# Other array shapes for four small matmuls, and scale, bias and gain in other places, in a hybrid RWKV-7 and Mamba-2 layer

## The chip, the cores and the metric

One core of one Trainium2 chip runs the whole program. The metric is the device time of one execution in microseconds, as the median over runs. The engines are TensorE (PE in the profile; its weight loads are PEld), VectorE (DVE), ScalarE (ACT), GpSimd (POOL) and SyncE (SP), whose queue issues the DMA transfers.

## The reference

One decoder layer runs over a prompt of 2048 tokens and eight sample tokens of 1024 features. All values are fp32.

```python
proj = x @ w_in                                   # 1024 -> 3336
pr = proj[..., :1792]; u = pr + (prev - pr) * mu  # prev: the row before
r, k, v, uw, ua, ug = split(u)                    # 3 x 512, 64, 64, 128
w_log = -softplus(-(w0 + tanh(uw) @ w_up)) - 0.5; decay = exp(-exp(w_log))
a = sigmoid(a0 + ua @ a_up); g = sigmoid(ug) @ g_up
# per head (8 heads of 64), step by step, S is the state:
S = S * w_t + (S @ ka_t) kb_t^T + v_t k_t^T;  y_t = S @ r_t
o_r = (group_norm(y) + sum(r * k * r_k) * v) * g
# Mamba-2: short convolution, dt = softplus(proj_dt + bias) with 8 heads,
# chunked scan, gate, RMS norm -> o_m
h = layer_norm(ALPHA * x + [o_r, o_m] @ w_out) * g1 + b1
y = layer_norm(ALPHA * h + square(relu(h @ w_ff1)) @ w_ff2) * g2 + b2
```

The states are outputs too.

## The kernel before

The prompt is cut into four blocks of 512 tokens; the sample rides with block 1. `project` multiplies a block by 27 tiles of `w_in`, 128 output features each and 8 for dt (`T_DT`). Weights and activations are split into a high part in fp32r and the rest (`split`: ACT copies, DVE or GpSimd subtracts), and `mm3` sums three fp32r matmuls: high by high, high by rest, rest by high. Small matmuls that are not split are plain fp32; the profile records each as two instructions. `pair` takes two heads through the low-rank projections and writes the scaled vectors to DRAM (`s_ar`, `s_bk`, `s_v`).

`mixers` then runs the recurrence in eight chunks of 64 steps per block. `rwkv` prepares one chunk: the score matmuls `pss` of `bk` and `ar` into two banks, one for each half of the partitions (four pairs of heads, two halves), a blocked inverse by `masked` and transposes, and the tiles `sc`, `xf`, `bt`, `uv`. `chain` carries the state `ST` from chunk to chunk: `pr` from scores by v plus `ar` by state, `pu`, then `pn`, `py` and the next state. `rwkv_post` and `mamba` do the rest of the mixing.

`tail` is the bulk of a block: the output projection in two halves (eviction L1257), the transposes `hT` of the normalised rows (L163) with `ln1` scale and bias (L1295, in ACT) and the split, then the MLP in `ff1` and the accumulation into `hs` (L1453). Two generators finish a block late: `late` normalises the old block and multiplies by the gain `ln2` (`gain`, L1175 and L1176, two DVE operations of 128x1024 for each of four row tiles, then the DMA to y_p), and `gain` does `ln1` for the rows that stay as the residual. `late` is stepped in the second half of the output projection and emptied ahead of the transposes.

`drive` mixes the bulk generators with the mixers of the next block by rates: mixers of block 0 run beside the projections of blocks 1 to 3, mixers of block b+1 beside the tail of block b. What is written in this order is only a priority: at build time a planner with a cost model places every instruction, each engine then runs its own list in order, and tiles come from pools with fixed numbers of buffers (`BUFS`; PSUM: three banks `psb`, one `psa`, two `psm`, one `psc`, one `psy`). `g4` holds the wide row tiles, the hidden tiles, the pair tiles and the gain vectors.

Of the kernel before, what the change touches and what calls it, by code (L numbers as in the profile page):

```python
# [18 lines left out]
FIRST = 4  # L19
POOLA, POOLO, POOLF = 4, 2, 0  # L20
# [6 lines left out]
BUFS = (("wr", 7), ("w", 8), ("act", 8), ("g4", 12), ("r", 2), ("blk", 4),  # L27
# [3 lines left out]
KT = 8  # L31
# [76 lines left out]
class K:  # L108
# [41 lines left out]
    def mm(self, out, l, r, start=True, stop=True):  # L150
        self.nc.tensor.matmul(out, l, r, start=start, stop=stop)  # L151
# [71 lines left out]
    def setup_mix(self):  # L223
# [51 lines left out]
        self.waup = c("waup", (128, 512))  # L275
        nc.sync.dma_start(self.waup, A["waup"])
# [49 lines left out]
    def wpieces(self, j, halves=(0, 1)):  # L326
        out = []
        w = TILES[j][1]
        for h in halves:
            if w == 128:  # L330
                src = self.A["w_in"][j if j < T_DT else j - 1, :, h * 512:(h + 1) * 512]
            else:
                src = self.A["w_dt"][:, h * 32:(h + 1) * 32]
            out.append(self.wpiece(src, (4, w)))
        return out

    def project(self, b, ahead):
# [13 lines left out]
        for j in range(NT):  # L351
            w = TILES[j][1]
            if b == 0 and j < len(self.first):
# [26 lines left out]
    def evict(self, b, j, mains):  # L380
        nc, st = self.nc, self.blkst[b]
        if j < T_DT:
# [22 lines left out]
            if j == T_UWA:  # L405
                nc.scalar.activation(u[0:64], u[0:64], AF.Tanh)
            elif j == T_UG:
# [11 lines left out]
        else:  # L419
            i = j - T_Z  # L420
            th = self.pair_tile()[0][:, :TB]
            for o, m, ps in mains:
# [4 lines left out]
                              th.rearrange("p (u t) -> p u t", u=4))  # L427

# [36 lines left out]
    def delta(self, b, mains):  # L465
        nc, st = self.nc, self.blkst[b]
        raw = self.pair_tile()[0]
        for o, m, ps in mains:
            nc.scalar.activation(raw[0:8, o:o + m], ps, AF.Copy)
        pt = self.ps("a", (128, 4, 8))  # L470
        for u in range(4):
            self.tr(pt[:, u, :], raw[0:8, u * 128:(u + 1) * 128])
        dt = self.sm("dt", [128, 4, 8], bufs=4)
        nc.vector.tensor_tensor(out=dt, in0=pt, in1=self.dtb.unsqueeze(1).to_broadcast([128, 4, 8]), op=ALU.add)
# [28 lines left out]
    def pair(self, b, hp):  # L503
# [22 lines left out]
        self.mm(pw, self.waup[0:64, cs], uwa[0:64])  # L526
        self.mm(pa, self.waup[64:128, cs], uwa[64:128])
# [15 lines left out]
        for u in range(4):  # L543
# [22 lines left out]
        nc.sync.dma_start(self.s_bk[b][:, 64:128, hp, :].rearrange("c p x -> p c x"),  # L566
                          BK[64:128].rearrange("p c a t -> p c (a t)"))
        for a in range(2):
            nc.sync.dma_start(self.s_bk[b][:, 0:64, hp, (1 - a) * 64:(1 - a) * 64 + 64].rearrange("c p x -> p c x"),
                              BK[0:64, :, a, :])  # L570
# [1007 lines left out]
```

## Time and profile before

| | us |
|---|---|
| median of three runs | 2901.62 (2898.83 to 2908.35) |
| the profiled execution | 2905.99 |
| its span, first to last instruction | 2904.2 |

The profiled execution is one run with the hardware profiler; the sums are made against its own time. Granted clock is the share of full speed that the throttle gave TensorE; its mean over the span was 0.985.

### The profile page before, as it was taken

How to read it: one execution, taken by the hardware profiler on the slowest of the kernel's cores; microseconds unless marked ns; L12 is line 12 of the kernel's file. 1: busy time of each engine (PE TensorE's matmuls, PEld its weight loads, DVE VectorE, ACT ScalarE, POOL GpSimd, SP SyncE). 2: the span in 40 equal slices, each digit the busy share in tenths (PEclk: the TensorE clock that was granted, in tenths of full speed). 3: DMA queues.
4: the chain of work that ended last, by engine and by line, in shares of the span. 5: the costliest groups of instructions: out<-in, count | busy, mean ns of one | idle time of the engine just before them, and what ended most of it. 6: DMA issues, size and time to landing. Idle time of an engine off the chain costs nothing.

```text
span 2904.2 us, 53242 instructions
## 1 busy us (share of the span) xinstructions
PE 2825.7 (97%) x19648; PEld 2331.7 (80%) x19648; DVE 1963.2 (68%) x4765; ACT 1249.2 (43%) x2391; POOL 356.6 (12%) x510
## 2 busy tenths in 40 slices
PE   9999999999999999999999999998999999899997
PEld 6798987777788777788888888887877878888886
DVE  6767868867857777686866666568766655754446
ACT  4454544543536333344544344335443334543332
POOL 2221212211221000001300000022000000300001
PEclk9999999999999999999999999999999999999999
DMA  6654654554645444355523344254343334433232
GB/s 191 182 174 122 176 179 139 165 175 136 178 144 162 129 124 119 114 160 176 175 89 106 116 122 120 76 174 165 114 137 110 108 106 162 164 99 94 91 100 71
DMA packets 334169, 395.34 MB, mean 136 GB/s; under 512 B 85518, under 2 KB 191588, under 8 KB 333900
## 3 DMA queue, kind: packets, MB, share of 16 engines
q1 hardware_dynamic: 333908, 391.94, 44.8%
q8 instruction: 154, 2.52, 0.4%
q14 instruction: 107, 0.88, 0.1%
HBM read 331.06 MB, written 60.81 MB: 135 GB/s over the span
## 4 chain that ended last, share of the span: by engine, by line
PE 83%; DVE 9%; DMA 4%; issue 2%; ACT 2%; SPq 0%; POOL 0%; DVEq 0%; ACTq 0%; POOLq 0%
PE psb L156 19%; PE psb L157 18%; PE psb L158 18%; PE psm L151 7%; PE psa L156 4%; PE psa L157 4%; PE psa L158 4%; PE psc L151 2%; PE psa L151 2%; PE psm L163 1%; PE psy L694 1%; PE psb L151 1%; DVE w L190 1%; DMA wr<-in_w_in_dram 1%; DVE g L1176 1%
## 5 line engine op out<-in xcount | busy, mean ns | idle before, releaser
L189 ACT ACTIVATE w<-wr 128x512 fp32r<-128x512 f32 (+1 forms) x840 | 521.0, 625 | 693.2 <-PE psb L158 272.3
L190 DVE TENSOR_TENSOR w<-wr,w 128x512 fp32r<-128x512 f32 x714 | 511.0, 722 | 255.7 <-ACT w L189 247.0
L156 PE MATMUL psb<-act,w 128*128 128x512 f32 (+3 forms) x1796 | 637.4, 356 | 5.7 <-ACT act L189 5.0
L157 PE MATMUL psb<-act,w 128*128 128x512 f32 (+3 forms) x1796 | 630.0, 351 | 0.0
L158 PE MATMUL psb<-act,w 128*128 128x512 f32 (+3 forms) x1796 | 628.3, 350 | 0.0
L156 PEld LDWEIGHTS psb<-act,w 128*128 128x128 f32 (+1 forms) x1796 | 337.9, 189 | 61.5 <-ACT act L189 6.3
L158 PEld LDWEIGHTS psb<-act,w 128*128 128x128 f32 (+1 forms) x1796 | 338.4, 189 | 51.4 <-issue 3.3
L157 PEld LDWEIGHTS psb<-act,w 128*128 128x128 f32 (+1 forms) x1796 | 339.1, 189 | 46.1 <-DVE act L190 1.3
L156 PE MATMUL psb<-w,g 128*128 128x512 f32 x788 | 315.7, 403 | 0.2 <-ACT w L189 0.2
L157 PE MATMUL psb<-w,g 128*128 128x512 f32 x788 | 312.4, 396 | 0.0
L158 PE MATMUL psb<-w,g 128*128 128x512 f32 x788 | 311.4, 395 | 0.0
L190 POOL TENSOR_TENSOR w<-wr,w 128x512 fp32r<-128x512 f32 (+1 forms) x126 | 181.5, 1445 | 564.6 <-ACT w L189 546.4
L1453 DVE TENSOR_TENSOR g<-psb,g 128x512 f32<-128x512 f32 x173 | 118.9, 688 | 158.2 <-PE psb L158 157.8
L156 PEld LDWEIGHTS psb<-w,g 128*128 128x128 f32 x788 | 148.0, 188 | 36.5 <-ACT w L189 0.6
L158 PEld LDWEIGHTS psb<-w,g 128*128 128x128 f32 x788 | 148.0, 188 | 34.5 <-issue 0.3
L157 PEld LDWEIGHTS psb<-w,g 128*128 128x128 f32 x788 | 148.4, 188 | 32.5 <-issue 0.2
L190 DVE TENSOR_TENSOR g<-r,g 128x256 fp32r<-128x256 f32 (+1 forms) x172 | 97.2, 565 | 87.4 <-ACT g L189 86.3
L1403 ACT ACTIVATE r<-psb 128x512 f32<-128x512 f32 (+2 forms) x130 | 63.3, 488 | 208.9 <-PE psb L158 205.7
L156 PE MATMUL psa<-act,w 128*128 128x256 f32 (+2 forms) x336 | 115.7, 344 | 0.0
L157 PE MATMUL psa<-act,w 128*128 128x256 f32 (+2 forms) x336 | 114.1, 340 | 0.0
L158 PE MATMUL psa<-act,w 128*128 128x256 f32 (+2 forms) x336 | 113.5, 338 | 0.0
L156 PE MATMUL psb<-g,w 128*128 128x264 f32 (+3 forms) x324 | 108.9, 336 | 1.2 <-DVE g L400 0.8
(376 smaller groups left out, 5237.2 us busy)
## 6 DMA issues: line engine op xcount, KB each, us to landing
wr<-in_w_ff_dram SPq DMA_DIRECT2D x512, 256.0 KB
wr<-in_w_in_dram SPq DMA_DIRECT2D x208, 256.0 KB
wr<-in_w_out_dram SPq DMA_DIRECT2D x112, 256.0 KB
lr<-d_l SPq DMA_DIRECT2D x256, 64.0 KB
s_m<-g SPq DMA_DIRECT2D x48, 256.0 KB
ms<-s_m SPq DMA_DIRECT2D x16, 768.0 KB
wr<-in_xT_dram SPq DMA_DIRECT2D x32, 256.0 KB
s_ar<-g SPq DMA_DIRECT2D x16, 512.0 KB
```

Source lines behind the costliest of these rows:

```text
L151: self.nc.tensor.matmul(out, l, r, start=start, stop=stop)
L156: nc.tensor.matmul(out, l[0], r[0], start=first, stop=False)
L157: nc.tensor.matmul(out, l[0], r[1], start=False, stop=False)
L158: nc.tensor.matmul(out, l[1], r[0], start=False, stop=last)
L163: self.nc.tensor.transpose(out, in_, self.cst[p0:p0 + k, o + p0:o + p0 + k])
L189: nc.scalar.activation(hi, raw, AF.Copy)
L190: (eng or nc.vector).tensor_tensor(out=lo, in0=raw, in1=hi.bitcast(F32), op=ALU.subtract)
L694: acc = lambda o, l, r, start, stop: nc.tensor.matmul(o, l, r, start=start, stop=stop, skip_group_check=True)
L1176: eng.tensor_tensor(out=h, in0=h, in1=b[:p], op=ALU.add)
L1403: nc.scalar.activation(rl, ps, AF.Relu)
L1453: self.nc.vector.tensor_tensor(out=h, in0=ps, in1=h, op=ALU.add)
```

## The change

- Low-rank projections: the weights `w_up` and `a_up` are held as two tiles each of 128 rows (the high part stacked on itself, the rest stacked on itself), the inputs as high part over rest (`stacked`), and `pair` sums two fp32r matmuls of 128 rows where it had one fp32 matmul of 64.
- dt: high part and rest of the eight weight columns stand side by side as 16 columns (`wdt`), so two matmuls a step do the work of three; `delta` adds the two groups of eight after the transpose. The sample adds them with one small matmul.
- Scores: the four times two matmuls go through `row`, which gives all but the first a high priority and ties each behind the one before; the first is placed behind a DVE memset of one element of the second bank (`held`), without a wait between the engines for it. The halves that `s_bk`, `s_v` and `sc` exchange are exchanged the other way round.
- pr: `ar` is copied into the free half of `sc` and the state into the free half of `uv`, and one matmul of 128 rows replaces two of 64 that were summed.
- Tail: odd k of the scale and bias are done by DVE. The old block's gain and output (`finish2`) leave `late` and are stepped as `later` ahead of the new block's gain, one step per `ff1`; the gain vectors of `ln1` are loaded after them. `g4` has 14 buffers for 12, in the room that a smaller DMA scratch leaves.

The diff, cut: the renamed halves, the sums in `delta` and the sample's own matmuls are left out.

```diff
-BUFS = (("wr", 7), ("w", 8), ("act", 8), ("g4", 12), ("r", 2), ("blk", 4),
+BUFS = (("wr", 7), ("w", 8), ("act", 8), ("g4", 14), ("r", 2), ("blk", 4),
...
+    def row(self, args, held):
+        prev = self.mm(*args[0])
+        self.tc.add_manual_dep(prev.ins, held.ins.name, mybir.DependencyInfo(
+            mybir.DependencyClass.NoSync, mybir.DependencyReason.DATA), reason="bank")
+        for a in args[1:]:
+            with self.tc.high_priority(RANK), self.tc.issue_after(prev.ins):
+                prev = self.mm(*a)
...
-        self.waup = c("waup", (128, 512))
-        nc.sync.dma_start(self.waup, A["waup"])
+        self.wup = []
+        for i in range(2):
+            raw = self.sb("wr", (128, 512))
+            for h in range(2):
+                nc.sync.dma_start(raw[64 * h:64 * h + 64], A["waup"][64 * i:64 * i + 64])
+            self.wup.append([self.mp.tile([128, 512], F32R, name=f"wup{i}{s}") for s in range(2)])
+            self.split(raw, *self.wup[i])
...
+    def wdt(self):
+        raw = self.sb("wr", (128, 512))[:, :64]
+        self.nc.sync.dma_start(raw, self.A["w_dt"])
+        t = self.sb("w", (128, 2, 512), F32R)[:, 0, :128].rearrange("p (k s c) -> p s k c", k=KT, s=2)
+        self.split(raw.rearrange("p (k c) -> p k c", k=KT), t[:, 0], t[:, 1])
+        return t.rearrange("p s k c -> p k s c")
...
-                    l = [pieces[k // 4][i][:, k % 4, :] for i in range(2)]
                     r = [act[k][:, i, o:o + n] for i in range(2)]
-                    self.mm3(ps[:w, :n], l, r, k == 0, k == KT - 1)
+                    if j == T_DT:
+                        l = pieces[:, k].rearrange("p s c -> p (s c)")
+                        self.mm(ps[:w, :n], l, r[0], k == 0, False)
+                        self.mm(ps[:w, :n], l, r[1], False, k == KT - 1)
+                    else:
+                        l = [pieces[k // 4][i][:, k % 4, :] for i in range(2)]
+                        self.mm3(ps[:w, :n], l, r, k == 0, k == KT - 1)
...
+    def stacked(self, u):
+        nc = self.nc
+        hl = self.sb("g4", (128, 2, 520), F32R)
+        W, a = hl[:, 0, :TB], hl[:, 1, :TB]
+        lo, hi = slice(0, 64), slice(64, 128)
+        for t, x, y in ((W, lo, hi), (a, hi, lo)):
+            nc.scalar.activation(t[x], u[x], AF.Copy)
+            nc.vector.tensor_tensor(out=t[y], in0=u[x], in1=t[x].bitcast(F32), op=ALU.subtract)
+        return W, a
...
         pw, pa = self.ps("a"), self.ps("b")
-        self.mm(pw, self.waup[0:64, cs], uwa[0:64])
-        self.mm(pa, self.waup[64:128, cs], uwa[64:128])
+        for p, w, x in ((pw, self.wup[0], uwa[0]), (pa, self.wup[1], uwa[1])):
+            self.mm(p, w[0][:, cs], x, True, False)
+            self.mm(p, w[1][:, cs], x, False, True)
...
         pss = [self.ps("m", (128, 4, 128)) for j in range(2)]
-        for hp in range(4):
-            for j in range(2):
-                self.mm(pss[j][:, hp, :], bk[H[j], hp, :], ar[H[j], hp].rearrange("p a t -> p (a t)"))
+        held = nc.vector.memset(pss[1][0:1, 0, 0:1], 0.0)
+        self.row([(pss[j][:, hp, :], bk[H[j], hp, :], ar[H[j], hp].rearrange("p a t -> p (a t)"))
+                  for hp in range(4) for j in range(2)], held)
...
         g2 = masked(x2, "m2")
+        for j in range(2):
+            nc.scalar.activation(sc[H[j], j, :, 0:64], ar[H[j], :, 0, :], AF.Copy)
...
         pr = self.ps("c", (128, 4, 64))
+        nc.scalar.activation(uv[H[0], 0], S[H[0]], AF.Copy)
+        nc.vector.tensor_copy(uv[H[1], 1], S[H[1]])
         for hp in range(4):
             for j in range(2):
-                self.mm(pr[H[1 - j], hp, :], sc[H[j], j, hp, 0:64], uv[H[j], j, hp, :], True, False)
-            for j in range(2):
-                self.mm(pr[H[1 - j], hp, :], ar[H[j], hp, 0, :], S[H[j], hp, :], False, True)
+                self.mm(pr[H[j], hp, :], sc[:, j, hp, 0:64], uv[:, j, hp, :])
...
-                nc.scalar.activation(raw, p[:, :n], AF.Identity, scale=self.par("g1", k), bias=self.par("b1", k))
+                if k % 2:
+                    nc.vector.tensor_scalar(out=raw, in0=p[:, :n], scalar1=self.par("g1", k), scalar2=self.par("b1", k),
+                                            op0=ALU.mult, op1=ALU.add)
+                else:
+                    nc.scalar.activation(raw, p[:, :n], AF.Identity, scale=self.par("g1", k), bias=self.par("b1", k))
...
-        g1 = self.affine(1)
-        gain = itertools.chain(*([self.gain(h, 128, *g1) for h in hs[:4]] +
-                                 ([self.gain(hs[4][0:8], 8, *g1)] if smp else [])))
+        def gains():
+            yield from self.later
+            g1 = self.affine(1)
+            for h in hs[:4]:
+                yield from self.gain(h, 128, *g1)
+            if smp:
+                yield from self.gain(hs[4][0:8], 8, *g1)
+        gain = gains()
...
         def finish():
             if nxt is not None:
                 yield from self.ln(hs[:4], [bs[:, i] for i in range(4)], 128)
+            if smp:
+                yield from self.ln_s(hs[4])
+        def finish2():
+            if nxt is not None:
                 for i in range(4):
                     yield from self.gain(hs[i], 128, *ab, rows[i])
             if smp:
-                yield from self.ln_s(hs[4])
                 yield from self.gain(hs[4][0:8], 8, *ab, A["y_s"])
-        self.late = finish()
+        self.late, self.later = finish(), finish2()
...
-    nc = bacc.Bacc("TRN2", target_bir_lowering=False, num_devices=1)
+    nc = bacc.Bacc("TRN2", target_bir_lowering=False, num_devices=1, dynamic_dma_scratch_size=256)
```

## Rows read from the trace of the kernel before

**Rows 1.** The page: the span, the busy time of each engine with its share of the span and its instructions, and the first line of the chain of work that ended last, by engine.

```profile
span 2904.2 us, 53242 instructions
...
PE 2825.7 (97%) x19648; PEld 2331.7 (80%) x19648; DVE 1963.2 (68%) x4765; ACT 1249.2 (43%) x2391; POOL 356.6 (12%) x510
...
PE 83%; DVE 9%; DMA 4%; issue 2%; ACT 2%; SPq 0%; POOL 0%; DVEq 0%; ACTq 0%; POOLq 0%
```

**Rows 2.** Busy time of each engine in two stretches (start:end, length, then busy us and instructions for each engine, then granted clock, DMA share and GB/s): in the projection of block 2, and from the MLP of one block into that of the next.

```profile
425.00:600.00 175.00, 171.68 (x1157) 130.15 (x1156) 137.51 (x339) 74.26 (x132) 36.24 (x70) 1.00 0.55 157
...
1850.00:2440.00 590.00, 578.97 (x4199) 477.11 (x4199) 385.86 (x966) 238.15 (x456) 49.30 (x47) 0.99 0.40 123
```

**Rows 3.** Groups of instructions on PE, different shapes apart (line, engine, operation, out<-in, rows*columns of the weights, shape, count | busy us, mean ns of one | idle time before, and what ended it): the score matmuls, and the low-rank matmuls of the sample.

```profile
L151 PE MATMUL psm<-ar,bk 64*128 64x128 f32 x512 | 58.0, 287 | 5.9 <-DVE xs L634 2.5 <-DMA bk<-s_bk 2.0 <-DVE sc L593 1.3
...
L151 PE MATMUL psm<-ms,waup 64*128 64x8 f32 x16 | 2.1, 255 | 0.0
```

**Rows 4.** Busy time in the projection stretch (0 to 850 us) of the instructions that read the tile waup alone.

```profile
0.00:850.00 850.00, 33.19 (x64) 9.42 (x64) 0.99 0.57 164
```

**Rows 5.** Timeline of PE around one low-rank group of block 0 (start us, duration us, engine, line, operation, tiles, shape, how many merged).

```profile
109.81 0.39 PE L157 MATMUL psb<-act,w 128*128 128x512 f32 x1
110.13 1.12 PE L151 MATMUL psa<-g,waup 64*128 64x512 f32 x2
111.18 0.50 PE L158 MATMUL psb<-act,w 128*128 128x512 f32 x1
111.52 0.39 PE L156 MATMUL psb<-act,w 128*128 128x512 f32 x1
```

**Rows 6.** Timeline of PE at the start of the dt tile of block 0.

```profile
100.64 0.39 PE L156 MATMUL psb<-act,w 128*8 128x512 f32 x1
100.87 0.40 PE L157 MATMUL psb<-act,w 128*8 128x512 f32 x1
```

**Rows 7.** Timeline of PE around one score group that is apart and one that is joined.

```profile
1041.43 1.16 PE L151 MATMUL psm<-ar,bk 64*128 64x128 f32 x8
1042.52 0.51 PE L158 MATMUL psa<-w,g 128*128 128x512 f32 x1
...
1082.37 1.16 PE L151 MATMUL psm<-ar,bk 64*128 64x128 f32 x16 [0.48 <-DMA bk<-s_bk]
1083.46 0.50 PE L156 MATMUL psb<-act,w 128*128 128x512 f32 x1
```

**Rows 8.** Timeline of PE around the product pr in three chunks: the first matmuls of one that runs into 64x64 matmuls of other tiles, with the bulk matmul behind it; the pn matmuls of another chunk, which have 128 rows and 64 columns, with what follows; the first and the next bulk matmul of one that stands alone.

```profile
259.78 0.51 PE L151 MATMUL psm<-xs,xs 64*64 64x64 f32 x10
...
261.15 0.38 PE L156 MATMUL psb<-g,w 128*128 128x256 f32 x1
...
350.64 0.69 PE L151 MATMUL psc<-uv,bt 128*64 128x64 f32 x16
351.15 0.64 PE L694 MATMUL psy<-sc,uv 128*64 128x64 f32 x16
...
988.67 0.33 PE L151 MATMUL psc<-uv,sc 64*64 64x64 f32 x4
...
989.74 0.50 PE L156 MATMUL psb<-act,w 128*128 128x512 f32 x1
```

**Rows 9.** The waits of PE (who waited for whom: us in total, times, longest us).

```profile
PE psb L163 <- DVE g L1257: 7.9, 3, 4.7
PE psm L151 <- DVE sc L593: 6.0, 5, 4.5
...
PE psa L163 <- DVE g L1257: 4.7, 2, 2.9
```

**Rows 10.** Timeline of all engines in two places ahead of transposes; in brackets the idle time of the engine before it and what ended it.

```profile
1455.15 1.21 DVE L1176 TENSOR_TENSOR g<-g,g 128x1024 f32<-128x1024 f32 x1
...
1456.35 0.67 DVE L593 TENSOR_TENSOR sc<-psm,cst 128x512 f32<-128x512 f32 x1
...
1457.08 1.12 PE L151 MATMUL psm<-xs,xs 64*64 64x64 f32 x16 [4.49 <-DVE sc L593]
...
2508.90 2.07 POOL L190 TENSOR_TENSOR w<-wr,w 128x512 fp32r<-128x512 f32 x1 [1.31 <-ACT w L189]
...
2510.06 4.20 DVE L1176 TENSOR_TENSOR g<-g,g 128x1024 f32<-128x1024 f32 x2
...
2514.65 0.69 PE L163 MATMUL psa<-cst,g 128*128 128x128 f32 x2 [2.91 <-DVE g L1257]
```

**Rows 11.** Busy time of each engine in stretches of 10 us; the number behind POOL is the granted clock of TensorE as a share of full speed.

```profile
230.00:240.00 10.00, 7.95 (x65) 7.67 (x64) 7.53 (x17) 4.24 (x11) 2.02 (x5) 0.83 0.89 261
...
1460.00:1470.00 10.00, 9.72 (x76) 7.50 (x75) 7.06 (x19) 6.21 (x15) 0.30 (x1) 0.51 0.22 55
...
2520.00:2530.00 10.00, 8.61 (x47) 7.68 (x45) 4.39 (x20) 7.55 (x16) 0.00 (x0) 0.60 0.70 221
```

**Rows 12.** Groups on ACT and DVE whose durations stand in for what is added or moved: the scale and bias on ACT, the copies of 64x256 on ACT and on DVE, and, from the page, the split's subtraction.

```profile
L1295 ACT ACTIVATE r<-psb,prm 128x256 f32<-128x256 f32 x42 | 22.4, 559 | 12.1 <-PE psb L163 9.3 <-DVE act L190 1.6 <-PE psa L163 1.1
...
L685 ACT ACTIVATE uv<-psc 64x256 f32<-64x256 f32 x32 | 12.1, 379 | 41.7 <-PE psc L151 41.3
...
L686 DVE COPY uv<-psc 64x256 f32<-64x256 f32 x32 | 13.1, 410 | 1.2 <-ACT uv L685 1.2
...
L190 DVE TENSOR_TENSOR w<-wr,w 128x512 fp32r<-128x512 f32 x714 | 511.0, 722 | 255.7 <-ACT w L189 247.0
```

More of the change, by code (lines that the diff above doesn't have):

```diff
@@ L19 @@
 FIRST = 4
+RANK = 4000
 POOLA, POOLO, POOLF = 4, 2, 0
@@ L150, in mm @@
     def mm(self, out, l, r, start=True, stop=True):
-        self.nc.tensor.matmul(out, l, r, start=start, stop=stop)
+        return self.nc.tensor.matmul(out, l, r, start=start, stop=stop)
+    def row(self, args, held):
[5 more added lines that the diff above has]
+                prev = self.mm(*a)
     def mm3(self, out, l, r, first, last):
@@ L351, in project @@
         for j in range(NT):
-            w = TILES[j][1]
-            if b == 0 and j < len(self.first):
+            w = 128 if j != T_DT else 16
+            if j == T_DT:
+                pieces = self.wdt()
+            elif b == 0 and j < len(self.first):
                 pieces = self.first[j]
@@ L406, in evict @@
                 nc.scalar.activation(u[0:64], u[0:64], AF.Tanh)
+                st[j] = self.stacked(u)
             elif j == T_UG:
@@ L631, in masked @@
             for hp, e in idx:
-                self.mm(p[H[e], hp, :], sc[H[e], 1 - e, hp, 0:64], x[H[e], hp, :])
+                self.mm(p[H[e], hp, :], sc[H[e], e, hp, 0:64], x[H[e], hp, :])
             o = xt()
@@ L924, in sample @@
         for hp in range(4):
-            self.mm(pw[:, hp, :], self.waup[0:64, hp * 128:(hp + 1) * 128], us[0:64, 0, :])
+            for i in range(2):
+                self.mm(pw[:, hp, :], self.wup[0][i][0:64, hp * 128:(hp + 1) * 128].bitcast(F32), us[0:64, 0, :], i == 0, i == 1)
         w = V6[:, 1]
@@ L933, in sample @@
         for hp in range(4):
-            self.mm(pa[:, hp, :], self.waup[64:128, hp * 128:(hp + 1) * 128], us[64:128, 0, :])
+            for i in range(2):
+                self.mm(pa[:, hp, :], self.wup[1][i][64:128, hp * 128:(hp + 1) * 128].bitcast(F32), us[64:128, 0, :], i == 0, i == 1)
         a = t(4, 8)
@@ L1071, in sample @@
         dd = t(2, 8)
-        nc.vector.tensor_scalar(out=dd[0:8, 0, :], in0=P[0:8, T_DT, :], scalar1=hb[0:8, 0:1], scalar2=None, op0=AD)
+        pd = self.ps("m", (128, 8))
+        self.mm(pd[0:8], self.con("s16", 0, 16), P[0:16, T_DT, :])
+        nc.vector.tensor_scalar(out=dd[0:8, 0, :], in0=pd[0:8], scalar1=hb[0:8, 0:1], scalar2=None, op0=AD)
         self.softplus(dd[0:8, 0, :], 8, 8)
@@ L1476, in body @@
             k.drain(smp)
-        k.late = iter(())
+        k.late = k.later = iter(())
         fills = []
@@ L1497, in body @@
             k.drive(k.nxt, "o", b, fills)
-        for _ in k.late:
+        for _ in itertools.chain(k.late, k.later):
             pass
```

33 lines of the change are left out of this document (16 added, 17 removed).

## Prediction

> **What bounds the kernel now.** I read the page first. TensorE (PE) is busy 2825.7 of the 2904.2 us, VectorE (DVE) 68% and ScalarE (ACT) 43%, and the chain that ended last runs 83% over PE [rows 1]. The table by stretches shows the same everywhere: 171.68 of 175 us in the stretch where DVE is fullest (137.51), 578.97 of 590 in a later one [rows 2]. So PE's instruction stream is the clock of this kernel, its idle time is only 2904.2 - 2825.7 = 78.5 us, and an edit pays by the PE time it takes out of the stream. Busy durations overlap, so I price a matmul by its step, the distance from its start to the next start, in the timeline of PE [rows 5 to 8]. The list of PE's waits [rows 9] and the timeline of DVE beside it [rows 10] come last, with the clock that PE was granted [rows 11]: they show where PE stands.
>
> **The change, part by part.**
>
> *Low-rank up-projections (pair).* Now two fp32 matmuls of 64 rows, recorded as two instructions each. A two-instruction group steps 1.05 us (110.13 to 111.18) [rows 5]. Over the projection all 64 are busy 33.19 us [rows 4]; the x2 row lasts 1.12 where its step is 1.05, so some 2 us of that are overhang and 31.2 us are steps. After: 4 matmuls of 128 rows for each of the 16 pairs, 64 in all, of the same shape as the bulk, which steps 0.23 [rows 6]: 14.9 us. Saved 16.3. The group also costs at its edges: 0.32 us from the bulk matmul before it and 0.34 from the one behind it to the next, where 0.23 is normal, about 0.2 a group [rows 5]; if nearly all groups stand alone, 5 us more go. Term **-21** (-16 to -24).
>
> *The dt tile.* Three matmuls become two for each of 8 steps. A matmul of 512 columns steps 0.23 (100.64 to 100.87) [rows 6], so a block saves 8 x 0.23 = 1.84; the sample block does it in two segments of about half the width and saves as much. 4 x 1.84 = **-7.4**. One weight load and one split fewer per block: not on the path.
>
> *Scores (rwkv).* 512 instructions are busy 58.0 us [rows 3]. Where the planner put both halves together, 16 instructions step 1.09 us (1082.37 to 1083.46), busy 1.16; where the two halves are apart, 8 alone take 1.09 too (1041.43 to 1042.52) [rows 7]. So halves on different row groups run side by side if they alternate, and the new helper forces that in all 32 chunks: 32 x 1.16 = 37.1. Saved 20.9. The edges of groups that are apart fall away too: with 1.16 for a chunk joined and 2.32 for one apart, 58.0 answers to 18 chunks apart, 18 x 0.2 = 3.6 us if each has an edge of its own; I take 2. Term **-23**. Bounds: 0, if the helper joins nothing, and -25.
>
> *The product pr (chain).* Now 32 instructions step 1.07 us (988.67 to 989.74). After: 16 of the form 128 rows by 64 columns, which step 0.51 (350.64 to 351.15) [rows 8]. 32 x 0.56 = 18 us saved at most. Today some of these groups run into other 64x64 groups without an edge: 259.78 to 261.15 is 48 instructions in 1.37 us [rows 8]. The new shape would have an edge of some 0.2 there. I take about half the chunks at 0.2: **-15** (-11.5 with an edge in every chunk, 18 - 32 x 0.2, to -18). The Trainium skill's TensorEngine Tiling (Array Packing), Key Properties, says that a change of tiling mode drains TensorE; by it every one of the 32 new shapes pays and the term is -11.5, while by the row at 259.78 only those that lost a neighbour of their own shape do, and the sum moves by 3.5 us.
>
> *Sample.* 16 instructions more of the form that was busy 2.1 us [rows 3], and one small fold: **+2**.
>
> *Work beside PE.* ACT gains two copies of 64x256 per chunk and one of the state, 96 x 0.38 = 36 us, and 10 half splits, and loses 32 scale-and-bias steps of 0.56. DVE gains 32 state copies at 0.41, 32 scale-and-bias steps, for which the nearest row is the 0.41 copy from PSUM, 10 split subtractions at up to 0.72, and 32 one-element memsets, between 0 and 0.41 [rows 12]. That is some 37 us of DVE, 1963 to 2000 us, about 71% of the new span: I cost it at nothing, because PE's stream covers it. In the fullest stretch [rows 2] DVE rises from 79% to some 85%; if the cover went, DVE's 37 us would be the price. The state copies are issued one chain step after the state and before pr; several mixer steps of bulk lie between. The first load of the up-projection weights becomes four half loads and two splits in the start, behind three tiles of weights already fetched: nothing.
>
> *Scale, bias and gain moved (tail).* The late gains of the old block (two ops of 1.2 us for each of four tiles) leave the place ahead of the transposes and are offered during the first up-projections. Today PE's transposes wait for the eviction L1257 7.9 + 4.7 us, and a score eviction L593 6.0 us [rows 9]; the timeline shows why: L593 starts at 1456.35 right behind a gain op (1.21 us at 1455.15) and PE, which had stood 4.49 us for it, starts again at 1457.08; at 2510.06 two gain ops take 4.20 us, beside a split on GpSimd, and PE then stands 2.91 [rows 10]. With it goes clock: the stretch 1460 to 1470 was granted 0.51, 2520 to 2530 0.60, after PE had stood [rows 11]; returning these two stretches to full level is worth about 9.72 x 0.49 + 8.61 x 0.40 = 8 us. Ceiling 18.6 + 8 = -27. Floor 0: the gain ops stay ready work that the planner can put into any gap of DVE, as the one at 1455 was. I take the wait tied to the gains directly, 12.6: **-12**. What is late next: y_p's output DMAs and the two loads of the next gain vectors come later on SP's queue, in front of weight loads; eight weight buffers of 12 matmuls x 0.23 = 2.8 us each cover 22 us of that. Holding the old tiles needs 4 old, 4 new, 2 vectors and 4 hidden tiles of g4, 14, and 15 where the sample tile is among them; one hidden tile may then wait for an output.
>
> *New waits.* Each score row now waits for two free banks and a DVE memset. The score matmuls wait 5.9 us in all today [rows 3]; I let that double (+6) and add 4 for gaps that a shorter stream uncovers: **+10** (0 to +30).
>
> Sum: -21 - 7.4 - 23 - 15 + 2 - 12 + 10 = -66.4. The profiled execution took 2905.99 us, its span 2904.2 and 1.8 around it that nothing here touches; it lies 4.4 above the median of the runs: 2905.99 - 66.4 = 2839.6, on the median 2835.
>
> **The rivals.**
>
> *The rows wait (slower).* PE is in order; a score row whose memset sits in DVE's queue behind gains or evictions stops the whole stream. For it: L593's wait at 1457.08 was 4.49 us of exactly that kind, and in the 10 us from 230, of which PE was busy 7.95, the granted clock was 0.83, 1.7 us lost [rows 10, 11]. The Trainium skill's TensorE: Matmul & The Clock Gate, Architectural detail, says that ACT and DVE are strict FIFO, which fits that row. Against it: the waits for DVE in [rows 9] come to 18.6 us in the whole span. To cancel 66 us and 0.3% (9 us), the 32 rows must stand 75 / 32 = 2.3 us each, or some 20 of them 2 us with 1.7 us of clock behind each. Then 2910 or more.
>
> *The saved steps come back as waits.* If DVE, the mixers' dependent steps and the loads pace more than the 78.5 us of idle time shows, half of the gain returns: 2901.6 - 33 = 2868. Against it: PE is full also where DVE is at 65% [rows 2].
>
> *The transposes' stalls go altogether.* Term -27 instead of -12, and no new waits: 2835 - 25 = 2810. For it: gain ops cost 2.1 us beside GpSimd's splits and would move to where those are rarer [rows 10].
>
> *The helper does not pair.* Without the -23: 2858.
>
> **How the numbers follow.** Chances: forecast 0.60 (its own range 2815 to 2862, the helper's rival at its end 0.08 beside it), half returned 0.13, stalls gone 0.12, rows wait 0.07. The range 2803 to 2880 takes in all but the rows' case and the outer parts of the others. This kernel's runs tell a difference from no change at about 0.3%. Faster by more than that is all but the rows' rival and a part of the returned half that returns more: 0.89; within it 0.05; slower 0.06.
>
> **What would show it.** The low-rank group gone from the 64-row forms and 64 new bulk-shaped steps of 0.23; dt with two instructions a step; every score group 16 long and 1.09 us; pr 16 instructions in about 0.51; PE's idle time near 75 us and PE's busy time near 2760. The list of waits should have L163 behind L1257 under 5 us and a new entry for PE behind a memset under 10. I am wrong if that entry is tens of us, if score groups stay at 8, or if the clock falls in more stretches than before.

## The result and the profile after

The changed kernel takes 2883.62 us (median, 2882.40 to 2884.64) against 2904.98 for the kernel before beside it: ratio 0.9928, interval 0.9912 to 0.9944. It is faster by 21 us where 66 were forecast, outside the forecast's range. Its profiled execution took 2883.41 us.

The page after, the lines of [rows 1]:

```profile
span 2881.6 us, 52238 instructions
...
PE 2788.4 (97%) x19114; PEld 2316.0 (80%) x19114; DVE 1995.2 (69%) x4873; ACT 1272.9 (44%) x2461; POOL 365.5 (13%) x508
...
PE 80%; DVE 10%; issue 4%; DMA 3%; ACT 2%; SPq 1%; POOL 0%; DVEq 0%; ACTq 0%; POOLq 0%
```

PE is busy 37 us less and idle 93.2 us instead of 78.5 (some 2760 and 75 were named as signs), and the trace has 17 stretches of the lower clock for 14 before, which was named as a sign of being wrong. I split the span of each trace in three: PE's idle time; what it loses to the lower clock (half of the busy time that overlaps the clock rows of the lower level, with the first 9 to 15 us, ahead of the first clock row, counted as lower); and the rest, its work at full level. Against the kernel before, in us of the profiled span:

| kernel | work | idle | clock | span |
|---|---|---|---|---|
| changed | -47.7 | +14.7 | +10.4 | -22.6 |
| forecast | -64.4 | -2, with the clock | | -66.4 |

So 17 us of the work that was to go are still there, and 25 us came back as idle time and lower clock. Where they came back is seen in the busy times by stretch (the columns as in [rows 2]): the projection, and the first tail, from the last statistics of block 0's out-projection to those of block 1's, in which the mixers of block 1 and then the sample block run beside the MLP. The kernel before:

```profile
0.00:785.20 785.20, 767.03 (x5170) 616.00 (x5171) 589.40 (x1454) 369.26 (x684) 173.22 (x334) 0.99 0.57 164
...
893.60:1422.30 528.70, 522.81 (x3679) 426.39 (x3679) 385.61 (x949) 230.92 (x442) 45.43 (x46) 1.00 0.48 143
```

The changed kernel:

```profile
0.00:754.10 754.10, 735.14 (x5008) 608.09 (x5009) 596.43 (x1483) 381.65 (x718) 180.06 (x332) 1.00 0.59 172
...
861.80:1407.20 545.40, 526.55 (x3618) 429.74 (x3616) 392.95 (x974) 239.30 (x456) 47.98 (x46) 0.98 0.45 138
```

The projection is 31.1 us shorter; the terms put some 38 there (low-rank, dt, and a quarter of scores and pr). The first tail has 61 matmuls fewer and is 16.7 us longer: PE stood 5.9 us in it before, 18.9 after, which is 13 of the 14.7 us of idle time, and the mean clock fell from 1.00 to 0.98, which costs 8.4 us where it cost nothing before. The list of PE's waits after, beside [rows 9]:

```profile
PE psb L166 <- ACT w L199: 13.6, 4, 8.8
PE psb L173 <- DVE g L1308: 10.4, 4, 3.4
PE psb L173 <- DVE r L1347: 6.0, 7, 1.4
PE psb L166 <- ACT act L199: 5.4, 1, 5.4
PE psm L152 <- issue: 5.4, 5, 1.7
...
PE psa L173 <- DVE g L1308: 4.3, 2, 2.5
```

The line numbers have moved: L1308 is the old L1257, L199 the split's copy, L173 the transposes. One stall is new and large, 8.8 us behind a weight split. The eviction L1308 holds the transposes for 14.7 us (12.6 before). The new DVE scale-and-bias L1347 holds them for 6.0, but that is hardly more than before, when the scale and bias on ACT held them for 5.3 in the list of the kernel before:

```profile
PE psa L163 <- ACT r L1295: 3.0, 4, 1.8
...
PE psb L163 <- ACT r L1295: 2.3, 2, 1.3
```

The clock behind the new stall, by tens of us:

```profile
1300.00:1310.00 10.00, 5.52 (x24) 4.13 (x22) 7.59 (x11) 6.29 (x10) 0.00 (x0) 1.00 0.39 101
1310.00:1320.00 10.00, 5.66 (x17) 4.21 (x17) 6.20 (x12) 3.79 (x7) 0.00 (x0) 0.53 0.84 289
1320.00:1330.00 10.00, 9.96 (x56) 7.91 (x56) 6.95 (x21) 4.18 (x9) 2.57 (x2) 0.79 0.03 7
```

### The profile page after: what moved, and what is told of

Same layout as the page of the kernel before. It is cut to its first block, busy times and chain, and to the rows that moved or that the text cites. A ratio compares the mean times of both kernels' runs of the same rounds, so it can differ in the third digit from the quotient of the medians.

```text
span 2881.6 us, 52238 instructions
## 1 busy us (share of the span) xinstructions
PE 2788.4 (97%) x19114; PEld 2316.0 (80%) x19114; DVE 1995.2 (69%) x4873; ACT 1272.9 (44%) x2461; POOL 365.5 (13%) x508
## 4 chain that ended last, share of the span: by engine, by line
PE 80%; DVE 10%; issue 4%; DMA 3%; ACT 2%; SPq 1%; POOL 0%; DVEq 0%; ACTq 0%; POOLq 0%
PE psb L166 18%; PE psb L167 18%; PE psb L168 18%; PE psm L152 7%; PE psa L166 4%; PE psa L167 4%; PE psa L168 4%; PE psc L152 2%; DVE w L200 1%; PE psa L152 1%; PE psb L152 1%; PE psm L173 1%; PE psy L741 1%; DVE lr L655 1%; DVE rX L656 1%
## 5 line engine op out<-in xcount | busy, mean ns | idle before, releaser
L199 ACT ACTIVATE w<-wr 128x512 fp32r<-128x512 f32 (+1 forms) x836 | 519.3, 627 | 632.7 <-PE psb L168 239.1
L166 PE MATMUL psb<-act,w 128*128 128x512 f32 (+2 forms) x1768 | 628.7, 357 | 6.4 <-ACT act L199 5.4
L167 PE MATMUL psb<-act,w 128*128 128x512 f32 (+2 forms) x1768 | 620.8, 352 | 0.1
L168 PE MATMUL psb<-act,w 128*128 128x512 f32 (+2 forms) x1768 | 617.0, 349 | 0.0
L166 PEld LDWEIGHTS psb<-act,w 128*128 128x128 f32 x1768 | 336.4, 191 | 54.4 <-ACT act L199 5.8
L168 PEld LDWEIGHTS psb<-act,w 128*128 128x128 f32 x1768 | 336.5, 190 | 46.3 <-DVE w L200 0.5
L167 PEld LDWEIGHTS psb<-act,w 128*128 128x128 f32 x1768 | 337.3, 191 | 42.9 <-DVE act L200 0.9
L200 POOL TENSOR_TENSOR w<-wr,w 128x512 fp32r<-128x512 f32 x124 | 187.2, 1515 | 690.9 <-ACT w L199 581.1
L655 DVE TENSOR_TENSOR lr<-rX,lr 128x4 f32<-128x4 f32 (+14 forms) x480 | 100.7, 210 | 10.7 <-DVE rX L656 0.2
```

What stands on the lines that cost most here:

```text
L166: nc.tensor.matmul(out, l[0], r[0], start=first, stop=False)
L167: nc.tensor.matmul(out, l[0], r[1], start=False, stop=False)
L168: nc.tensor.matmul(out, l[1], r[0], start=False, stop=last)
L199: nc.scalar.activation(hi, raw, AF.Copy)
L200: (eng or nc.vector).tensor_tensor(out=lo, in0=raw, in1=hi.bitcast(F32), op=ALU.subtract)
L655: nc.vector.tensor_tensor(out=row, in0=X[:, :, s + 1:16], in1=row, op=ALU.mult)
```

## The experiments

Differences are (ratio - 1) x 2903 us against the kernel before that ran beside each. A kernel has the buffers of the changed one (14 g4 tiles, the small DMA scratch), but for the two of "Order and hold" that are made from the kernel before. Work, idle time and clock are those of the one profiled execution, the times are medians of all runs.

**Shapes or tail.** Three kernels take the change apart, and a fourth offers the side steps faster.

> The four array-shape changes (low-rank, dt, score rows, pr) with the buffers of the changed kernel, and the scale, bias and gains left where they were. The prediction's terms put this at 54 to 56 us under the kernel before (-66.4 without the -12 of the moved scale, bias and gains). My theory after the result: the shapes take about 47 us of work off PE, a stall of 9 us and some 10 us of clock come in the first tail, and the moved gains gave nothing; so about 21 us under the kernel before, the same as the changed kernel within 6 us. Rival 1, the moved steps cost time (transposes behind the new DVE eviction, the steps around transposes are 8 us longer): this kernel is 8 us or more faster than the changed one. Rival 2, the moved steps gave their 12 us and the shapes gave only 10: this kernel is 12 us slower than the changed one.

> Only the moved scale, bias and gains, with the buffers of the changed kernel, on the kernel before. The prediction's term: 12 us faster than the kernel before (0 to 27). My theory: nothing that can be told from none, within 6 us, because the gains stay ready work that lands in front of the evictions anyway. Rival 1: 8 us slower, as the eight longer steps around the transposes would say.

> The changed kernel with the gains of the old block back ahead of the transposes; scale and bias of odd k stay on DVE. My theory: within 6 us of the changed kernel, and the same 8.8 us stall in front of the first activation loads of block 1, since nothing before that place differs. Rival: the held gains are what is worth something, and this kernel is 8 us or more slower than the changed one, with the transposes' waits behind evictions at 12 us or more against 18 in the changed kernel.

```diff
-RATE_M0, RATE_M, RATE_S = 0.2, 0.23, 0.35
+RATE_M0, RATE_M, RATE_S = 0.2, 0.23, 0.45
```

> The changed kernel with one number moved: the steps of the mixers and of the sample block are offered at 0.45 in place of 0.35 during the first tail, so that the sample's four state loads are issued ahead of the eight activation loads of block 1 and no longer between them. My theory (the stall of 8.8 us at 1305 comes from that collision and takes the clock down behind it for 13.7 us): the stall and its half clock go, 12 to 16 us faster than the changed kernel. Rival (the shorter stream is paced by its side work, whatever the order): the stall shows up in another place of the same tail and the time stays within 5 us of the changed kernel.

Shapes alone: 2883.94 us, ratio 0.9936 [0.9919, 0.9953]. Tail alone: 2896.73, 0.9976 [0.9960, 0.9992]. Gains put back: 2886.17, 0.9942. Faster offer: 2886.39, 0.9938 [0.9918, 0.9958]. So the moved scale, bias and gains are worth 7 us (2 to 12) alone, where my theory had nothing and the forecast 12, and nothing that can be told beside the shapes, as expected; both kernels without the held gains have the same stall (8.65 us at 1301, 8.98 at 1303). My theory of the collision fell with the fourth: its four state loads do stand ahead of the activation loads, its 8.8 us stall is gone, and 6.69 us at 802 (PE waiting for a tile xs of DVE) and 4.83 us at 1279 (PE's transposes waiting for the load of d_y) stand in its place. The rival was right there.

**The four shapes, one by one.**

> The low-rank up-projections alone (with the buffers of the changed kernel). The prediction's term is -21 us. The steps counted in the trace of the changed kernel say 14 us of PE work. Theory A (a few places cost the rest, above all the score rows that wait for two banks and DVE): all of the 14 us is seen, no new waits. Theory B (any shortening of the stream uncovers the side work, whatever part makes it): about half of it comes back as waits and half clock, 7 us faster.

> The dt tile alone (with the buffers of the changed kernel). The prediction's term is -7.4 us; counted steps in the changed kernel say 5.6 us of PE work. Theory A: 5 to 7 us faster. Theory B: 3 us faster, not told from none.

> The score rows alone, with the one-element memset and the forced row of 16 (with the buffers of the changed kernel). The prediction's term is -23 us, with up to +10 us of new waits, 13 us faster. Counted steps in the changed kernel say 22.8 us of PE work. Theory A: this part carries the new waits: the waits of PE rise by 10 us or more and the half clock with them, so 5 us faster or less. Theory B: 11 us faster, its waits rise no more than those of the other parts for each us of work.

> The product pr alone, stacked to 128 rows, with its three copies and the swapped halves (with the buffers of the changed kernel). The prediction's term is -15 us. Counted steps in the changed kernel say 4 us of PE work, since 12 us of its own steps come back in part as edges at the 64x64 matmuls that it used to run into. Theory A: 4 us faster, not told from none. Theory B: 2 us faster. If the prediction's term were right and the loss lay elsewhere: 11 to 18 us faster.

| part alone | time, us | ratio, interval | work | idle | clock |
|---|---|---|---|---|---|
| low-rank | 2891.19 | 0.9958 [0.9941, 0.9975] | -17.1 | +5.5 | +3.0 |
| dt | 2910.99 | 1.0028 [1.0014, 1.0042] | -8.1 | +7.3 | +3.4 |
| score rows | 2910.58 | 1.0036 [1.0022, 1.0049] | -17.1 | +18.3 | +3.5 |
| pr | 2896.07 | 0.9982 [0.9969, 0.9995] | -3.1 | +1.9 | -9.2 |

The work adds up (-45.4, against -45.3 for the four shapes together and -47.7 for all), the times don't. (The profiled execution of low-rank lies 6 us above its median, that of the kernel before 4 us, so a row's three terms differ from its time.) Two parts that take 8 and 17 us off PE make the kernel slower by 8 and 10 us. Neither theory had that: the score rows carry waits, as theory A said, but dt does too. Low-rank came out between the two theories, pr near both. With dt and with the score rows the loss is in the first tail (545.4 and 546.9 us long; 528.7 before, 534.9 with low-rank, 526.5 with pr). The new buffers were not run alone; low-rank and pr have them too, without such a tail, so they aren't what makes it long. The timeline of the score rows alone shows the rival "the rows wait" in one place:

```profile
1124.44 0.06 DVE L600 MEMSET psm<- 1x1 f32 x1
...
1140.09 0.69 DVE L749 TENSOR_TENSOR q<-q,q 128x512 f32<-128x512 f32 x1 [11.64 <-DMA q<-s_bv]
...
1141.30 0.68 DVE L756 TENSOR_TENSOR q<-psm,q 128x512 f32<-128x512 f32 x1
...
1142.08 2.08 PE L152 MATMUL psm<-ar,bk 64*128 64x128 f32 x16 [8.77 <-issue]
```

The memset takes one bank at 1124; the other bank that the row needs is, as far as the rows tell, the one that L756 empties, which on DVE stands behind L749 and a load that landed late. PE stands 8.77 us, and the row then runs at half clock, 2.08 us where [rows 7] have 1.16. Why that load took 10 us isn't shown.

**Order and hold.** The sample block's steps ahead of the mixers, on the changed kernel and on the one before; the memset away; the faster offer on the kernel before.

```diff
-                fills[0] = [itertools.chain(fills[0][0], smp[0]), "m", b + 1, RATE_S]
+                fills[0] = [itertools.chain(smp[0], fills[0][0]), "m", b + 1, RATE_S]
```

> The changed kernel with the sample block's steps offered ahead of the mixers of block 1 in the first tail and no longer behind them, so that its state loads are far from the activation loads of block 1. My theory now: the changed kernel loses its time in the first tail, where the sample block's steps (small loads and stores that other steps wait for) stand in the queues between the mixers' and the bulk's steps; the 8.8 us stall at 1305 and its half clock go, the first tail becomes 8 to 15 us shorter, 2868 to 2876. Rival (whichever way the side steps are placed, about as much waiting comes back, since the mixers and the sample together take the time that this stretch has): the first tail stays within 5 us and so does the whole.

> The same swap of order on the kernel before: the sample block's steps ahead of the mixers of block 1, and nothing of the change. It is the control: the kernel before stood only 6 us in its first tail. My theory: no room for a gain there, so within 6 us of the kernel before, or slower by up to 10 if the placement of its steps was a lucky one. Rival: it gains as much as the changed kernel does by the swap, and then the first tail's loss has nothing to do with the change.

```diff
-        self.tc.add_manual_dep(prev.ins, held.ins.name, mybir.DependencyInfo(
-            mybir.DependencyClass.NoSync, mybir.DependencyReason.DATA), reason="bank")
...
-        held = nc.vector.memset(pss[1][0:1, 0, 0:1], 0.0)
+        held = None
```

> The changed kernel without the one-element memset that takes the second bank ahead of a score row; the row of 16 is forced as before. If the early hold of a bank makes the new waits (the score rows alone had a stall of 8.8 us before a row), the waits of PE before score rows fall by 5 to 8 us and the time with them, to about 2876. Rival: the row then waits for the second bank in its middle instead, and the time stays within 5 us.

> The kernel before with the steps of the mixers and the sample block offered at 0.45 in place of 0.35 in the first tail, and nothing of the change. It shows what another placement of the same steps is worth without any change of the work. My theory (the first tail is sensitive to where the side steps fall, and the kernel before had them well placed): 5 to 15 us slower than the kernel before. Rival (placement is worth nothing in a stream that is full): within 4 us.

Sample first: 2903.95 us on the changed kernel (ratio 1.0007 [0.9996, 1.0018]), 2918.69 on the one before (1.0060 [1.0045, 1.0074]). My theory missed: the swap only moves the mixers to the end of the tail, and the changed kernel loses 20 us by it (38 us idle in the first tail). Faster offer on the kernel before: 2910.05, 1.0023 [1.0012, 1.0034], 7 us slower with the same work. In its profile none of the loss lies in the first tail as defined above (528.9 us long): 4.5 us lie ahead of it, with a wait of 5.42 us, and the rest behind. So where the same side steps are offered is worth 7 to 20 us (7 and 17 on the kernel before), and the kernel before had a good placing. Without the memset: 2879.26, 0.9923 [0.9910, 0.9936], 4.4 us faster than the changed kernel by the medians and 1.5 by the ratios, and not in the way that was expected. PE's work rises by 10 us (25 of 32 rows are cut behind their second matmul, as the timeline shows), while idle falls by 6.8 and the clock's loss by 7.5:

```profile
1098.64 0.48 PE L152 MATMUL psm<-ar,bk 64*128 64x128 f32 x2
1099.05 0.69 PE L152 MATMUL psc<-uv,sc 128*64 128x64 f32 x16
...
1109.15 1.16 PE L152 MATMUL psm<-ar,bk 64*128 64x128 f32 x14
```

**The rows of block 1.** What the first tails have in common is a later side chain. After the start of the tail (the last projection weight's load) the block's last store of the mixers comes at 405 us in the kernel before, 437 with the score rows alone, 436 in the changed kernel.

```diff
+        if b == 1:
+            for a in args:
+                self.mm(*a)
+        else:
+            held = nc.vector.memset(pss[1][0:1, 0, 0:1], 0.0)
+            self.row(args, held)
```

> The changed kernel with its score rows in all blocks but block 1, whose mixers run beside the first tail; there the sixteen score matmuls are left to the planner as in the kernel before, without the memset. Theory (the rows slow the side chain of this block, so that the sample block's state loads fall between the next activation loads): the last store of the mixers comes back to about 405 us after the start of the tail, the state loads stand ahead of the activation loads again, the stall of 8.8 us goes, and the first tail loses 12 to 20 us for 4 to 5 us more of PE work: 2866 to 2876. Rival (any shorter stream uncovers the same waiting in this tail): the first tail stays at 540 us or more and the time within 4 us of the changed kernel or slower.

> The kernel before with the score rows in block 1 alone (and the buffers of the changed kernel). Theory: all of the loss that the rows alone showed (9 us slower, for 17 us less work) is in the first tail, so this kernel is slower than the kernel before by 9 to 15 us, and its first tail is 12 to 18 us longer. Rival: the rows lose everywhere a little, and a quarter of them is within 4 us of the kernel before.

> The changed kernel without any score rows (the score matmuls left to the planner in all blocks). Theory: PE's work rises by 17 to 20 us, and the first tail gives back 12 to 20: within 6 us of the changed kernel, so the rows gave the change nothing. Rival: the rows are worth their 17 to 23 us, and this kernel is at 2900 or more.

> As the first kernel of this call, and without the one-element memset that holds the second bank. The changed kernel without the memset was 4 us faster than with it, with 10 us more of PE work, because 25 of its 32 rows were cut in two by bulk matmuls, and less waiting. If most of what the memset cost was the late chain of block 1, it is now worth its work, and this kernel is 2 to 6 us slower than the first one. Rival: the hold costs waits in every block, and this kernel is 3 to 5 us faster.

Rows in all blocks but 1: 2878.28, 0.9915 [0.9899, 0.9931]. Rows in block 1 alone on the kernel before: 2916.88, 1.0050 [1.0031, 1.0068]. No rows: 2885.38, 0.9944. Rows but in block 1, no memset: 2884.56, 0.9942. The second is as the theory said: a quarter of the rows costs 15 us, its first tail is 17 us longer, with the stall before a row again (8.35 us). The first is half a hit: the last store is back at 412 us and the 8.8 us stall is gone, but the tail is still 544.6 us long, with 4.50 us before the transposes that wait for d_y. Something else still held the sample block back. The third came out within 6 us of the changed kernel, as expected, but its tail gives back 3.9 us and not 12 to 20: over the whole span the rows save 19.6 us of work and cost 11.7 us of idle time and 6.1 of clock. The fourth is 6 us slower than the first (2 to 6 were expected), so with these rows the memset is worth its waits, while on the changed kernel it wasn't.

**The fold.** In the kernel before, the sample's dt is stored to memory and read back spread over the partitions early. SP's queue there (start, duration of issue):

```profile
1154.64 0.33 SPq L1077 DMA_DIRECT2D d_dt<-ms  x1
1163.89 1.23 SPq L1080 DMA_DIRECT2D ms<-d_dt  x2
```

That is 369 and 379 us after the start of the tail. In the changed kernel the one small matmul that adds the two groups of eight dt columns (the fold) stands ahead of it, and the timeline is

```profile
1247.34 0.20 PE L152 MATMUL psm<-sproj,cst 16*8 16x8 f32 x2
...
1247.57 0.21 DVE L1123 TENSOR_SCALAR ms<-psm,ms 8x8 f32<-8x8 f32 x1 [0.95 <-PE psm L152]
...
1251.95 0.41 SPq L1128 DMA_DIRECT2D d_dt<-ms  x1
1252.40 2.78 SPq L1139 DMA_DIRECT2D d_bc<-m  x4
1259.66 1.30 SPq L1131 DMA_DIRECT2D ms<-d_dt  x2
...
1263.13 0.75 DVE L1159 TENSOR_SCALAR m<-m,ms 128x1024 f32<-128x1024 f32 x1 [5.87 <-DMA ms<-d_dt]
...
1306.95 1.21 DVE L1167 TENSOR_REDUCE lr<-m 128x8 f32<-128x1024 f32 x1
1308.08 4.29 DVE L200 TENSOR_TENSOR act<-wr,act 128x512 fp32r<-128x512 f32 x7
1308.19 1.09 SPq L1068 DMA_DIRECT2D d_y<-lr  x2
1309.37 0.54 SPq L322 DMA_DIRECT2D wr<-s_o  x1
1309.96 0.90 SPq L206 DMA_DIRECT2D wr<-in_w_ff_dram  x2
...
1314.34 1.65 PE L166 MATMUL psb<-w,g 128*128 128x512 f32 x3 [8.82 <-ACT w L199]
```

Read it from the top: the fold runs 493 us after the start of the tail, so the store and the load of dt come 127 to 128 us later than before, and SP issues nothing between 1255.2 and 1259.66, when the load goes out. DVE stands 5.87 us for it. The four state steps end with L1167 at 1308.16; SP issues the store d_y right then, with the weight loads that PE needs behind it in the queue, and seven splits of activations stand behind L1167 on DVE. The chain that ended last passes through the splits, not the store; the weight load goes out as the third split ends:

```profile
1308.08 1.89 DVE act L200 x3
1309.96 3.68 DMA wr<-in_w_ff_dram
1313.66 0.64 ACT w L199
```

PE stands 8.82 us, and half clock follows. The late store of d_dt is no accident of one kernel: in the nine kernels that have the fold in this place behind the mixers it goes out 479 to 500 us after the start of the tail, and in the nine that don't have it there, 337 to 375 (the two with the sample block first aside).

```diff
                 nc.vector.tensor_copy(self.sproj[:w, j, :], banks[1][:w, 256:264])
+                if j == T_DT:
+                    pd = self.ps("a", (128, 8))
+                    self.mm(pd[0:8], self.con("s16", 0, 16), self.sproj[0:16, j, :])
+                    nc.vector.tensor_copy(self.sproj[0:8, j, :], pd[0:8])
```

(and the sample reads sproj as in the kernel before).

> The changed kernel with the score rows in all blocks but block 1, and with the fold matmul of the sample block's dt done at the end of block 1's dt projection, on another bank, and no longer in the sample block's steps. Theory (the fold held the sample block's state steps back by 9 us): d_dt is stored at about 370 us after the start of the tail as in the kernel before, the last state load is back at about 516 us, the stall before the d_y transposes goes, the first tail is 528 to 535 us long, and the kernel takes 2862 to 2870 us. Rival (the first tail is simply full of side work now): first tail 540 us or more, 2875 to 2882 us.

> The changed kernel with the early fold alone, the score rows in all blocks as they were. Theory: the last state load comes 9 us earlier (535 us after the start of the tail), still between the activation loads, so the stall of 8.8 us shrinks by some us but does not go: 2876 to 2882 us. Rival 1: the fold was the whole cause and this kernel is as fast as the other of this call. Rival 2: it makes no difference, within 3 us of the changed kernel's 2883.6.

Early fold with the rows of block 1 left to the planner: 2872.88 us, 0.9891 [0.9875, 0.9908]. Its theory missed: the first tail is 541.2 us long, as the rival had it, and only 3.4 of the 5.4 us that it gains on the same kernel with the late fold lie there. Early fold alone on the changed kernel: 2870.94, 0.9886 [0.9872, 0.9901], the fastest of all and 12.7 us faster than the changed kernel (12.2 by the ratios). Rival 1 was right: the fold alone does it, and the rows of block 1 then cost nothing that can be told. The store of d_dt is back at 368 us, the last state load comes 9 us earlier (534, between activation loads as expected), and no wait above 1.7 us takes its place until the transposes at 1387. SP's queue with the early fold:

```profile
1117.42 0.30 SPq L1130 DMA_DIRECT2D d_dt<-ms  x1
1143.51 1.52 SPq L1133 DMA_DIRECT2D ms<-d_dt  x2
...
1294.34 1.09 SPq L1072 DMA_DIRECT2D d_y<-lr  x2
...
1299.85 3.26 SPq L206 DMA_DIRECT2D wr<-in_w_ff_dram  x4
```

and its first tail, which is 11.6 us shorter than the changed kernel's (7.3 us of idle time and 4.6 of clock, about the stall and the half clock behind it):

```profile
858.90:1392.70 533.80, 522.26 (x3616) 426.06 (x3615) 394.48 (x973) 236.99 (x456) 50.09 (x46) 0.99 0.46 141
```

The stall goes with either of the two, the late fold or the rows of block 1; but where the rows of block 1 alone were taken away, 4.50 us before the transposes of d_y came in its place. Moving the fold also lets the planner place everything anew. That a part of the 12.7 us is such a placing can't be ruled out; that the gain lies where the stall was speaks against it.

## Why the prediction was wrong

Two steps failed most, the place of the fold and the work of pr, by about 12 us each.

**Sample, +2.** The fold was priced as one small matmul on PE. Its price was its place: a step that needs a bank and PE, put ahead of a store and a load that other queues wait for. Measured by moving the fold it is 12.7 us in the changed kernel, and 5.4 (7 by the ratios) where the rows of block 1 are left to the planner. The prediction followed the DMAs of the moved tail steps to their queue, and not those of this chain.

**pr, -15.** Of the 21 groups that stay 16 long, 18 step 0.61 or 0.62 and not 0.51; the other 11 are cut, mostly into 2 and 14:

```profile
561.52 0.69 PE L152 MATMUL psc<-uv,sc 128*64 128x64 f32 x16
562.13 0.50 PE L167 MATMUL psb<-act,w 128*128 128x512 f32 x1
...
679.60 0.33 PE L152 MATMUL psc<-uv,sc 128*64 128x64 f32 x2
...
680.29 0.68 PE L152 MATMUL psc<-uv,sc 128*64 128x64 f32 x14
```

Counted start to start the steps of pr fall from 38.1 to 26.3 us, and those of the 64x64 groups (xs, xs) that it used to run into rise from 36.9 to 44.8: 4 us in all. A part of that rise is the score rows' (xs is 42.7 with pr alone, 39.9 with the score rows alone). The part alone took 3.1 us of work off and was 5 us faster (1 to 9). The forecast took the edge for half the chunks, and for the new group alone; the neighbours pay one as well. So even the end of the term with an edge in every chunk, -11.5, was too large. The Trainium skill's TensorEngine Tiling (Array Packing), Key Properties, has every change of the tiling mode drain the array. The trace agrees with it in the steps of 0.61 for 0.51.

**Low-rank, -21.** The 64 steps are 22.1 us and not 14.9. In the bulk a group of two does step 0.46, but about a third of the groups stand behind the fp32 pair of the k norm and step 0.86 to 0.97, and another third beside other shapes step 0.54 to 0.67:

```profile
42.99 0.63 PE L152 MATMUL psa<-g,wup 128*128 128x512 f32 x2
43.45 0.39 PE L167 MATMUL psb<-act,w 128*128 128x512 f32 x1
...
686.46 1.03 PE L152 MATMUL psb<-g,wup 128*128 128x512 f32 x2
687.41 0.68 PE L152 MATMUL psc<-r,xf 64*64 64x64 f32 x16
```

The part alone is 12 us faster (7 to 17) for 17 us of work.

**dt, -7.4, and scores, -23.** Their own work was sized well: 8.1 us less with dt alone; all 32 score groups are 16 long and 27 of them step 1.09, 38.9 us for 61.7 counted start to start. For the scores that was in part luck. The prediction read 18 chunks apart from the busy time; counted, 10 were apart, and of the 22 joined ones only 4 stepped 1.09 while 13 stepped 1.67 or 1.68. And here too the neighbours pay: with the score rows alone the unchanged xs and pr rise by 3.0 and 1.9 us, and the work falls by 17.1, not 23. As times, both terms failed. Alone they made the kernel slower by 8 and 10 us. The scores have the bank that a row waits for; dt has its late fold (d_dt at 487 us, and 4.35 us of waiting before the transposes of d_y), but dt alone with an early fold was not run. Within the change the rows were worth 2 us by the medians, 5 by the ratios (2885.38, 0.9944 without them).

**New waits, +10.** Idle time rose by 14.7 us where this term and the tail's -12 together had it fall by 2, and not at the place named: the entry behind a memset is 2.3 us, and the largest part is a weight load behind DVE's late state steps. The rival "the rows wait" was right as a mechanism in two kernels, 8.8 and 8.4 us at one place each; in the changed one no row stands so long, though the rows cost it 11.7 us of idle time elsewhere. The clock wasn't in this term; it lost 10.4 us more.

**Tail, -12.** The wait that was to go below 5 us, L163 behind L1257, is 14.7. The wait for L593 did go (6.0 to 0.9 us), but with the shapes alone too (1.1). Within the change the term was the floor of 0 that was named; its reason, that the gains remain ready work for any gap of DVE, is argued and not shown.

**DVE and ACT at nothing** holds for their busy time (69% and 44%). What was forgotten beside it is order: L1159 stood 5.87 us, and seven splits stood behind L1167. The Trainium skill's TensorE: Matmul & The Clock Gate, Architectural detail, has DVE and ACT strictly in order. The trace agrees: DVE stood 2.34 us for a state load ahead of L1159 at 1303.16, while ACT had done its half of the first of those seven splits at 1301.3.

With the early fold the balance is work -47.4, idle +7.3, clock +6.8, span -33.3 us. So of the 44 us that are missing in the changed kernel's span 17 are work (by the parts alone, pr 12, scores 6, low-rank 4, with 5 gained elsewhere), 11 are the fold's place, and 16 are idle time and lower clock that remain. Of that idle time 5.5 us lie in the first tail, where the transposes at its end now wait 6.8 us for evictions:

```profile
1389.60 0.69 PE L173 MATMUL psb<-cst,g 128*128 128x128 f32 x2 [2.89 <-DVE g L1310]
...
1392.52 0.69 PE L173 MATMUL psa<-cst,g 128*128 128x128 f32 x2 [2.23 <-DVE g L1310]
```

This wait was 0.3 us in the kernel before, 1.6 with the shapes alone and 5.0 with the tail alone, so the tail's moved steps may have a part in it. Why it came, and the rest of the 16 us, stays open.

## What to carry to other kernels

A saved matmul step pays only where nothing is made late by it: before pricing a tiny added instruction by its duration, follow what it feeds through stores, loads and in-order queues, and ask how early that chain ran before. Parts that each shorten PE can each make the kernel slower, so measure them one by one, compare the stretches, and look in the one that grew for the first step that is late. A helper that needs two banks at once trades PE time for waits, and which of the two weighed more changed here from kernel to kernel.

## What the runs showed that was not expected

The same work placed otherwise made the kernel before slower by 7 us (offered at 0.45; 5 to 15 were expected) and 17 us (sample first; at most 10 were), as much as most terms of the forecast. A row of 16 score matmuls at the lower clock took 2.08 us where it takes 1.16 at the full one.
